# One splitter for each weight chunk, and small loads from another queue, in a three-layer mixture-of-experts program

## The chip, the cores and the metric

The kernel runs on one core of a Trainium2 chip. The metric is the device time of one execution in microseconds (us), the median of several runs.

## The reference

256 tokens of width 1024 in fp32 go through three layers. The first two form one block: a conditioning vector gives shift, scale and gate of each layer, a token mixer follows and then a mixture of experts. The third is a second block with another mixer.

```python
def first_block(x, c, ...):
    cond = jax.nn.silu(c)
    for layer in range(DEPTH):                        # 2
        mod = (cond @ ada_w[layer] + ada_b[layer])[:, None, :]
        shift1, scale1, gate1, shift2, scale2, gate2 = jnp.split(mod, 6, axis=-1)
        h = _rms(x, norm1_w[layer]) * (1 + scale1) + shift1
        ...
            y = _even_mixer(h, ...)                   # layer 0: window attention and gated linear attention
        ...
            y = _odd_mixer(h, ...)                    # layer 1: block attention
        x = x + gate1 * y
        h = _rms(x, norm2_w[layer]) * (1 + scale2) + shift2
        x = x + gate2 * _hier_moe(h, ...)             # 4 groups of 8 experts, hidden width 512
    return x

def second_block(x, attn_norm, w_in, ...):
    ...
        h = rmsnorm(x, attn_norm[layer])
        proj = h @ w_in[layer]
        ...
        o_nsa = nsa_mixer(...)                        # attention over compressed, selected, window keys
        o_hg = hgrn2_mixer(hg_q, hg_f, hg_i, lb)
        ...
        mixed = (gate_nsa * (o_nsa.astype(x.dtype) @ w_br_nsa[layer]) +
                 gate_hg * (o_hg @ w_br_hg[layer]))
        x = x + mixed @ w_out[layer]
        x = x + hier_moe(rmsnorm(x, ffn_norm[layer]), ...)
    return rmsnorm(x, final_norm)
```

## The kernel before, in words

One class, Net, writes the whole program. The stages follow each other: the even mixer (about 20 to 170 us of the trace), its experts, the odd mixer (about 684 to 835), its experts, the second block's mixer (about 1322 to 1545), its output projection and experts, and the last norm.

**Weights.** Almost all bytes are weights. They go into a ring of 19 slots of 1 MB (128 partitions x 2048 fp32). `plan` queues a load; `pump` (L182 to L194) issues queued loads on SP (SyncE) for as long as slots are free, with `dma_start` at L194. A slot is free when the last reader of the weights in it is done, and SP waits there.

**Splitting.** The mixers' matmuls run as three passes of a rounded format (fp32r), so each operand is a high part and a low part. For weights `prep` (L441) does this in chunks of two rows of blocks: ScalarE (ACT) casts 128x1024 to the high part `wh` at L461; VectorE (DVE) subtracts for the first half of the low part `wl` at L462, GpSimd (POOL) for the second half at L463, each 128x512. There are 120 such chunks, all in the mixers and the projections behind them; 112 are of this size, the others narrower. The high and low parts go to slots of the ring or to two buffers `wx`. `slab` (L468) takes one prepared chunk at a time and gives PE (TensorE) its matmuls (L258). The expert stages use their weights directly, without this split.

**Order.** Within a mixer `weave` (L213) interleaves generators: the projections (`stream`), the attention, the recurrent part. What a generator writes down lands on each engine's queue in that order, and each engine works through its queue in order. Copies out of PSUM go through `copy` (L249 on ACT, L251 on DVE), splits of activations through L254 (ACT) and L255 (DVE), transposes through `tr` (L268). In the attention of the second block L1284 to L1287 scale the exponentials of a row by the reciprocal of their sum, on DVE. In the odd mixer L1054 to L1063 are the softmax (L1058 the exponential on ACT, L1063 the scaling on DVE). L408 scales a selection matrix with the norm's coefficients at the start of a mixer, L631 applies a per-head norm, L798 gates the linear attention's output, L379 is a tiny power on POOL for the norms.

**Small loads.** 27 loads of constants and small weights stand on ACT's queue where a generator reaches them: `router` (L1619 to L1622, four loads, called in each of the three mixers' `stream`), `second_setup` (L1156, eleven loads, called in the odd mixer behind `router`), `nsa_prep` (L1165 and L1166, the two compression weights, into a slot of the ring), `hgrn` (L1335, the table `lvm`) and L1590 (the last norm's weight). A few loads of the first setup and of the biases stay on ACT in both kernels.

Of the kernel before, what the change touches and what calls it, by code (L numbers as in the profile page):

```python
# [9 lines left out]
FT = mybir.dt.float32  # L10
# [9 lines left out]
P = 128  # L20
D = 1024
KC = D // P
# [100 lines left out]
class Net:  # L123
# [322 lines left out]
    def prep(self, most=9):  # L446
        nc = self.nc
        while self.cq and len(self.ready) < min(most, len(self.wbufs) - 1):
            key, k, last = self.cq[0]
            if key not in self.live:  # L450
                self.pump()
                if key not in self.live:
                    return
            self.cq.pop(0)
            w = self.live[key]
            n = w.shape[2]
            src = w[:, k:k + 2]
            buf = self.wbufs[self.wi]
            self.wi = (self.wi + 1) % len(self.wbufs)
            wh, wl = (buf[:, 1024 * i:1024 * i + 2 * n].rearrange("p (k n) -> p k n", k=2) for i in range(2))  # L460
            nc.scalar.copy(wh, src)  # L461
            nc.vector.tensor_sub(wl[:, 0], src[:, 0], wh[:, 0].bitcast(FT))  # L462
            nc.gpsimd.tensor_sub(wl[:, 1], src[:, 1], wh[:, 1].bitcast(FT))  # L463
            self.ready.append((wh, wl))
            if last:
                self.done(key)
# [678 lines left out]
    def second_setup(self, g):  # L1145
        nc, A = self.nc, self.A
        self.S = {}
        for nm, src, shape in (
                ("k_rope", A["k_rope"], [P, 2 * T]), ("k_ropec", A["k_ropec"], [64, 60]), ("k_rot", A["k_rot"], [P, P]),
                ("k_csel", A["k_csel"], [30, P]), ("k_vmask", A["k_vmask"], [P, 512]),  # L1150
                ("pos", A["cmp_pos_2"][0].rearrange("(l q) d -> l (q d)", q=2), [16, P]),
                ("k_cmp", A["k_cmp"], [P, 64]), ("k_causal", A["k_causal"], [P, T]), ("k_scan", A["k_scan"], [P, T]),
                ("hn", A["hg_norm_2"].to_broadcast([P, P]), [P, P]),
                ("ll", A["hg_lb_logits_2"].rearrange("l (h p) -> (l h) p", p=P), [8, P])):
            self.S[nm] = g.tile(shape, FT, name=nm)
            nc.scalar.dma_start(self.S[nm], src)  # L1156

    def nsa_prep(self, g):
        nc, A = self.nc, self.A
# [2 lines left out]
        co, si = rp[:, :T], rp[:, T:]  # L1162
        vmk = vmk.rearrange("p (a b c) -> p a b c", a=4, b=2)
        wc = N["wc"]
        nc.scalar.dma_start(wc[:, 0], A["w_cmp_k_2"][0].rearrange("(l p) e -> p l e", p=P))  # L1165
        nc.scalar.dma_start(wc[:, 1], A["w_cmp_v_2"][0].rearrange("(l p) e -> p l e", p=P))  # L1166
        kr, vr = N["kr"], N["vr"]
        nc.gpsimd.memset(kr, 0.0)
        yield (0.0, 3.0)
        p = self.psum((P, 16))  # L1170
# [34 lines left out]
        p = self.psum((P, 64))  # L1205
# [10 lines left out]
        for b in range(2):  # L1216
            for gg in range(2):
                for par in range(2):
                    src = ks[64 * gg:64 * gg + 64, b]
# [98 lines left out]
    def hgrn(self, g, q8):  # L1318
        nc, A = self.nc, self.A
        q4 = lambda i: q8[i // 2][:, 1024 * (i % 2):1024 * (i % 2) + 1024]  # L1320
        h4 = lambda i: q4(i).rearrange("p (h t) -> p h t", h=4)
        k, b, q = (h4(i) for i in range(3))
# [9 lines left out]
        f = exs[0]  # L1332
        self.H = dict(k=k, b=b, q=q, v=v, gs=gs, f=f)
        lvm = g.tile([P, 7, 64], U32, name="lvm")
        nc.scalar.dma_start(lvm, A["k_levels"])  # L1335
        scan, ll = self.S["k_scan"], self.S["ll"]
        self.hn = self.S["hn"]
        nc.gpsimd.memset(att, 0.0)
# [1 line left out]
        p = self.psum((P, 8))  # L1340
# [72 lines left out]
        for t in range(NT):  # L1413
            p = self.psum()
# [6 lines left out]
        for c in range(3):  # L1421
            r0, t = 64 * (c % 2), c // 2
            p = self.psum()
# [9 lines left out]
        for t in range(NT):  # L1433
            po = self.psum()
            for h in range(4):
                o = po[:, P * h:P * h + P]
# [15 lines left out]
        for t in range(NT):  # L1452
            p = self.psum()
# [8 lines left out]
    def second(self, coeffs):  # L1462
        nc, tc = self.nc, self.tc
        with tc.tile_pool(name="sec", bufs=1, reuse_waits="tile") as g:
# [98 lines left out]
            def stream():  # L1563
# [23 lines left out]
                yield from branch(self.o[2:], 1)  # L1587
                self.release(3, reserve=3)
                coeffs()
                nc.scalar.dma_start(self.rows[1], self.A["final_norm_2"].rearrange("(o n) -> o n", o=1).to_broadcast([P, D]))  # L1590
                yield (5.0, 0.0)
                m = [(self.mx[0][:, k], self.mx[1][:, k]) for k in range(8)]
                yield from self.out_half(m[:4], False)
                yield from self.out_last(m[4:], False)

            self.weave(self.nsa_prep(g), self.nsa_attn(g, sc), self.hgrn(g, q8), stream())
        self.release(6)

# [15 lines left out]
    def router(self, l):  # L1614
        nc = self.nc
        wg, bg, we, be = self.moe_args(l)[0]
        wr = self.cp.tile([P, KC, 36], FT, name="wr", tag="wr")
        br = self.cp.tile([P, 36], FT, name="br", tag="br")
        nc.scalar.dma_start(wr[:, :, 0:4], wg.rearrange("(p k) n -> p k n", k=KC), allow_slow_non_contiguous=True)  # L1619
        nc.scalar.dma_start(wr[:, :, 4:36], we.rearrange("(p k) n -> p k n", k=KC), allow_slow_non_contiguous=True)  # L1620
        nc.scalar.dma_start(br[:, 0:4], bg.to_broadcast([P, 4]))
        nc.scalar.dma_start(br[:, 4:36], be.to_broadcast([P, 32]))  # L1622
        self.wr, self.br = wr, br

    def route_setup(self):
# [448 lines left out]
```

## Time and profile before

| | us |
|---|---|
| runs | 2068.37, 2071.49, 2070.86 (median 2070.86) |
| profiled execution, its own time | 2067.69 |
| its span in the trace | 2065.9 |
| PE busy | 1897.2 (92%) |
| DVE busy | 822.9 (40%) |
| ACT busy | 458.3 (22%) |
| POOL busy | 309.8 (15%) |
| read from memory | 722.48 MB, 350 GB/s over the span |

The shares are averages over stages that differ, so the profile is read by stretches of time. In a timeline row the first number is the start in us, the second the duration, "xN" a count of like instructions in a row, and the bracket the idle time of that engine just before and what ended it. "PE ps L258 <- DVE slot L462" reads: PE's instruction of L258 waited for DVE's of L462.

### The profile page before, as it was taken

The numbers are of one execution on the slowest core, as the hardware profiler recorded it, in microseconds if no ns is written. First come the engines' busy times: TensorE is split into PE (matmuls) and PEld (weight loads), VectorE is DVE, ScalarE is ACT, GpSimd is POOL, SyncE is SP. The second block draws the span as 40 slices with busy tenths as digits, with TensorE's granted clock in tenths as the row PEclk, the third lists the DMA queues.
The fourth block names the chain that finished last, engine by engine and source line by source line (L and its number), as shares of the span: only waits on it lengthen the run. The fifth ranks groups of instructions, "written<-read, shape, count | busy, mean of one in ns | idle before, by whom it ended". The sixth has DMA issues, their size and how long they took to land.

```text
span 2065.9 us, 25147 instructions
## 1 busy us (share of the span) xinstructions
PE 1897.2 (92%) x10032; PEld 1022.1 (49%) x10032; DVE 822.9 (40%) x1553; ACT 458.3 (22%) x838; POOL 309.8 (15%) x245
## 2 busy tenths in 40 slices
PE   6898999998989989999999889998899999999987
PEld 3655444343333657544433334586788443344333
DVE  3666433232322657623322222467666323222222
ACT  1424211111110443311111111254543111111111
POOL 1331000000000424000000000242443000000000
PEclk8998999999999999999999999999999999999999
DMA  8796999999999956799999999931357999999997
GB/s 314 274 312 251 375 422 421 420 421 422 421 420 405 367 211 242 303 401 421 421 421 421 421 421 421 342 106 42 131 191 268 379 421 421 420 421 421 421 421 287
DMA packets 157541, 725.29 MB, mean 351 GB/s; under 512 B 25305, under 2 KB 43087, under 8 KB 85225
## 3 DMA queue, kind: packets, MB, share of 16 engines
q1 hardware_dynamic: 139216, 716.84, 86.4%
q10 hardware_dynamic: 18201, 6.76, 1.3%
q8 instruction: 82, 1.34, 0.3%
q14 instruction: 42, 0.34, 0.0%
HBM read 722.48 MB, written 1.07 MB: 350 GB/s over the span
## 4 chain that ended last, share of the span: by engine, by line
DMA 23%; PE 19%; DVE 3%; issue 3%; ACT 2%; ACTq 0%; POOL 0%; POOLq 0%; SPq 0%; DVEq 0%
PE ps L258 18%; DMA slot<-moe_w 8%; DMA slot<-w_gate 5%; DMA slot<-w_up 4%; DMA slot<-w_down 2%; DMA more<-w_down 2%; DMA more<-w_up 2%; PE ps L268 1%; DVE slot L1287 1%; ACT slot L1275 1%; DMA slot<-w_in 0%; ACT slot L461 0%; DVE slot L462 0%; DVE hh L1861 0%; DVE wx L462 0%
## 5 line engine op out<-in xcount | busy, mean ns | idle before, releaser
L258 PE MATMUL ps<-slot,xg 128*64 128x512 f32 x2952 | 700.2, 599 | 47.5 <-DMA slot<-moe_w 34.3
L258 PEld LDWEIGHTS ps<-slot,xg 128*64 128x64 f32 x2952 | 225.0, 138 | 490.2 <-issue 381.2
L258 PE MATMUL ps<-slot 128*128 128x256 f32 (+8 forms) x2230 | 370.2, 327 | 11.5 <-DVE slot L462 9.0
L258 PE MATMUL ps<-slot,ht 128*64 128x512 f32 (+1 forms) x1592 | 341.7, 570 | 4.9 <-ACT ht L249 4.9
L258 PEld LDWEIGHTS ps<-slot 128*128 128x128 f32 (+3 forms) x2230 | 300.0, 186 | 72.2 <-issue 16.0
L1861 DVE SCALAR_TENSOR_TENSOR hh<-sg,ws,ps 128x512 f32<-128x512 f32 x48 | 54.3, 1130 | 603.6 <-PE ps L258 349.1
L258 PEld LDWEIGHTS ps<-slot,ht 128*64 128x64 f32 x1592 | 113.8, 137 | 198.1 <-issue 183.2
L1882 POOL TENSOR_TENSOR yl<-sg,yh 128x512 fp32r<-128x512 f32 (+1 forms) x68 | 82.4, 1211 | 862.5 <-ACT yh L1881 862.5
L463 POOL TENSOR_TENSOR slot<-slot 128x512 fp32r<-128x512 f32 (+2 forms) x108 | 163.5, 1531 | 279.5 <-ACT slot L461 247.3
L1908 DVE TENSOR_TENSOR x<-x,ps 128x512 f32<-128x512 f32 x180 | 113.6, 680 | 43.7 <-PE ps L258 41.5
L462 DVE TENSOR_TENSOR slot<-slot 128x512 fp32r<-128x512 f32 (+2 forms) x108 | 105.7, 992 | 57.3 <-ACT slot L461 54.6
L258 PEld LDWEIGHTS ps<-u,slot 128*128 128x128 f32 x864 | 105.6, 195 | 23.4 <-issue 17.0
L461 ACT CAST slot<-slot 128x1024 fp32r<-128x1024 f32 (+2 forms) x108 | 106.5, 1020 | 46.4 <-PE ps L258 24.8
L258 PE MATMUL ps<-u,slot 128*128 128x256 f32 (+1 forms) x864 | 111.0, 287 | 3.5 <-DVEq L1743 3.5
L1880 DVE TENSOR_TENSOR sg<-ps,ga 128x512 f32<-128x512 f32 (+1 forms) x68 | 44.9, 660 | 166.1 <-PE ps L258 155.8
L1857 ACT ACTIVATE sg<-ps 128x512 f32<-128x512 f32 x48 | 28.7, 597 | 325.7 <-PE ps L258 325.7
L1881 ACT CAST yh<-sg 128x512 fp32r<-128x512 f32 (+1 forms) x68 | 40.3, 593 | 251.7 <-DVE sg L1880 251.7
L258 PE MATMUL ps<-yh,pg 128*128 128x512 f32 (+1 forms) x204 | 85.5, 421 | 0.7 <-ACT yh L1881 0.7
L249 ACT COPY ht<-ps 128x512 f32<-128x512 f32 x48 | 28.1, 585 | 252.1 <-PE ps L268 251.9
L258 PE MATMUL ps<-yl,pg 128*128 128x512 f32 (+1 forms) x204 | 78.8, 389 | 4.3 <-POOL yl L1882 4.0
L399 ACT ACTIVATE xg<-ps,cf 128x256 f32<-128x256 f32 (+1 forms) x72 | 39.0, 542 | 172.6 <-PE ps L258 172.6
L1933 POOL TENSOR_TENSOR slot<-x,rows 128x512 f32<-128x512 f32 x2 | 2.6, 1276 | 460.2 <-DVE x L1929 460.2
(333 smaller groups left out, 1555.0 us busy)
## 6 DMA issues: line engine op xcount, KB each, us to landing
slot<-moe_w SPq DMA_DIRECT2D x376, 1024.0 KB, 19.8
slot<-w_gate SPq DMA_DIRECT2D x59, 1024.0 KB, 19.8
slot<-w_down SPq DMA_DIRECT2D x55, 1024.0 KB, 19.8
slot<-w_up SPq DMA_DIRECT2D x54, 1024.0 KB, 19.8
slot<-ada_w SPq DMA_DIRECT2D x48, 1024.0 KB, 9.0
slot<-w_in SPq DMA_DIRECT2D x20, 1024.0 KB, 7.4
slot<-odd_w_in SPq DMA_DIRECT2D x12, 1024.0 KB, 17.0
more<-w_up SPq DMA_DIRECT2D x10, 1024.0 KB, 16.1
```

The costliest lines, as they stand in the source:

```text
L249: self.nc.scalar.copy(out, in_)
L258: self.nc.tensor.matmul(out, lhsT=lhsT, rhs=rhs, start=start, stop=stop)
L399: self.nc.scalar.activation(out, p, AF.Identity, scale=a, bias=nb[:, k:k + 1])
L461: nc.scalar.copy(wh, src)
L462: nc.vector.tensor_sub(wl[:, 0], src[:, 0], wh[:, 0].bitcast(FT))
L463: nc.gpsimd.tensor_sub(wl[:, 1], src[:, 1], wh[:, 1].bitcast(FT))
L1857: nc.scalar.activation(sg, ps, AF.Silu)
L1861: nc.vector.scalar_tensor_tensor(ha.rearrange("s k p -> s p k"), st["sg", p].rearrange("s (p k) -> s p k", k=4), st["ws", p], ps.rearrange ...
L1880: nc.vector.tensor_mul(y, ps, self.ga[:, sl])
L1881: nc.scalar.copy(yh, y)
L1882: nc.gpsimd.tensor_sub(yl, y, yh.bitcast(FT))
L1908: nc.vector.tensor_add(self.x[:, t, sl], self.x[:, t, sl], ps)
```

## The change

The split of a chunk's low part becomes one DVE subtraction over the whole chunk (128x1024) in place of one half on DVE and one on POOL. The 27 small loads named above are issued by SP in place of ACT. Nothing else differs; lines behind L463 have numbers lower by one in the changed kernel.

```diff
--- before.py
+++ after.py
@@ -459,8 +459,7 @@
             self.wi = (self.wi + 1) % len(self.wbufs)
             wh, wl = (buf[:, 1024 * i:1024 * i + 2 * n].rearrange("p (k n) -> p k n", k=2) for i in range(2))
             nc.scalar.copy(wh, src)
-            nc.vector.tensor_sub(wl[:, 0], src[:, 0], wh[:, 0].bitcast(FT))
-            nc.gpsimd.tensor_sub(wl[:, 1], src[:, 1], wh[:, 1].bitcast(FT))
+            nc.vector.tensor_sub(wl, src, wh.bitcast(FT))
             self.ready.append((wh, wl))
             if last:
                 self.done(key)
@@ -1153,7 +1152,7 @@
                 ("hn", A["hg_norm_2"].to_broadcast([P, P]), [P, P]),
                 ("ll", A["hg_lb_logits_2"].rearrange("l (h p) -> (l h) p", p=P), [8, P])):
             self.S[nm] = g.tile(shape, FT, name=nm)
-            nc.scalar.dma_start(self.S[nm], src)
+            nc.sync.dma_start(self.S[nm], src)
 
     def nsa_prep(self, g):
         nc, A = self.nc, self.A
@@ -1162,8 +1161,8 @@
         co, si = rp[:, :T], rp[:, T:]
         vmk = vmk.rearrange("p (a b c) -> p a b c", a=4, b=2)
         wc = N["wc"]
-        nc.scalar.dma_start(wc[:, 0], A["w_cmp_k_2"][0].rearrange("(l p) e -> p l e", p=P))
-        nc.scalar.dma_start(wc[:, 1], A["w_cmp_v_2"][0].rearrange("(l p) e -> p l e", p=P))
+        nc.sync.dma_start(wc[:, 0], A["w_cmp_k_2"][0].rearrange("(l p) e -> p l e", p=P))
+        nc.sync.dma_start(wc[:, 1], A["w_cmp_v_2"][0].rearrange("(l p) e -> p l e", p=P))
         kr, vr = N["kr"], N["vr"]
         nc.gpsimd.memset(kr, 0.0)
         yield (0.0, 3.0)
@@ -1332,7 +1331,7 @@
         f = exs[0]
         self.H = dict(k=k, b=b, q=q, v=v, gs=gs, f=f)
         lvm = g.tile([P, 7, 64], U32, name="lvm")
-        nc.scalar.dma_start(lvm, A["k_levels"])
+        nc.sync.dma_start(lvm, A["k_levels"])
         scan, ll = self.S["k_scan"], self.S["ll"]
         self.hn = self.S["hn"]
         nc.gpsimd.memset(att, 0.0)
@@ -1587,7 +1586,7 @@
                 yield from branch(self.o[2:], 1)
                 self.release(3, reserve=3)
                 coeffs()
-                nc.scalar.dma_start(self.rows[1], self.A["final_norm_2"].rearrange("(o n) -> o n", o=1).to_broadcast([P, D]))
+                nc.sync.dma_start(self.rows[1], self.A["final_norm_2"].rearrange("(o n) -> o n", o=1).to_broadcast([P, D]))
                 yield (5.0, 0.0)
                 m = [(self.mx[0][:, k], self.mx[1][:, k]) for k in range(8)]
                 yield from self.out_half(m[:4], False)
@@ -1616,10 +1615,10 @@
         wg, bg, we, be = self.moe_args(l)[0]
         wr = self.cp.tile([P, KC, 36], FT, name="wr", tag="wr")
         br = self.cp.tile([P, 36], FT, name="br", tag="br")
-        nc.scalar.dma_start(wr[:, :, 0:4], wg.rearrange("(p k) n -> p k n", k=KC), allow_slow_non_contiguous=True)
-        nc.scalar.dma_start(wr[:, :, 4:36], we.rearrange("(p k) n -> p k n", k=KC), allow_slow_non_contiguous=True)
-        nc.scalar.dma_start(br[:, 0:4], bg.to_broadcast([P, 4]))
-        nc.scalar.dma_start(br[:, 4:36], be.to_broadcast([P, 32]))
+        nc.sync.dma_start(wr[:, :, 0:4], wg.rearrange("(p k) n -> p k n", k=KC), allow_slow_non_contiguous=True)
+        nc.sync.dma_start(wr[:, :, 4:36], we.rearrange("(p k) n -> p k n", k=KC), allow_slow_non_contiguous=True)
+        nc.sync.dma_start(br[:, 0:4], bg.to_broadcast([P, 4]))
+        nc.sync.dma_start(br[:, 4:36], be.to_broadcast([P, 32]))
         self.wr, self.br = wr, br
 
     def route_setup(self):
```

How it moves the instructions, at three places.

POOL in the second block's mixer (`slot` and `wx` are the buffers of the split chunks; L1383 and L1540 belong to the recurrent part). Before:

```order
L463 TENSOR_TENSOR wx<-slot,wx 128x512
L463 TENSOR_TENSOR slot<-slot 128x512 x4
L1383 TENSOR_TENSOR slot<-slot 128x16x32
L1383 TENSOR_TENSOR slot<-slot 128x32x16
L463 TENSOR_TENSOR wx<-slot,wx 128x512
L463 TENSOR_TENSOR slot<-slot 128x512 x2
L1383 TENSOR_TENSOR slot<-slot 128x64x8
L463 TENSOR_TENSOR slot<-slot 128x512
L1383 TENSOR_TENSOR slot<-slot 128x128x4
L463 TENSOR_TENSOR slot<-slot 128x512
L463 TENSOR_TENSOR wx<-slot,wx 128x512
L463 TENSOR_TENSOR slot<-slot 128x512
```

Now:

```order
L1223 COPY kd<-slot 64x256 x4
L1382 TENSOR_TENSOR slot<-slot 128x16x32
L1382 TENSOR_TENSOR slot<-slot 128x32x16
L1382 TENSOR_TENSOR slot<-slot 128x64x8
L1382 TENSOR_TENSOR slot<-slot 128x128x4
L1539 TENSOR_TENSOR slot<-slot,hn 128x512 x2
L1382 TENSOR_TENSOR slot<-slot 128x256x2
```

The subtractions are gone from POOL's queue, and what is left there, L1383 (now L1382) and L1540 (now L1539), follows directly. On DVE each L462 stands at its old place with 128x1024 in place of 128x512.

ACT in the odd mixer, behind the copies of `ga` and the four router loads (k_rope to ll are the constants of `second_setup`). Before:

```order
L1156 DMA k_rope<-k_rope 128x512
L1156 DMA k_ropec<-k_ropec 64x60
L1156 DMA k_rot<-k_rot 128x128
L1156 DMA k_csel<-k_csel 30x128
L1156 DMA k_vmask<-k_vmask 128x512
L1156 DMA pos<-cmp_pos 16x128
L1156 DMA k_cmp<-k_cmp 128x64
L1156 DMA k_causal<-k_causal 128x256
L1156 DMA k_scan<-k_scan 128x256
L1156 DMA hn<-hg_norm 128x128
L1156 DMA ll<-hg_lb_logits 8x128
L254 CAST slot<-ps 128x256 x3
```

Now, from the copies on:

```order
L249 COPY slot<-ps 128x512
L249 COPY ga<-ps 128x512 x2
L254 CAST slot<-ps 128x256 x3
L1057 ACTIVATE sc,den<-sc,mx 128x128
L1057 ACTIVATE sc,den<-sc,mx 128x256
L461 CAST slot<-slot 128x1024 x2
L249 COPY pT<-ps 128x384
```

The 15 loads stood between the copies and the casts L254; now the casts follow the copies. On SP these 15 stand behind the first of four loads of ada_w.

SP at the start of the second block's mixer (w_in, w_br_nsa and w_br_hg are the mixer's weights, lvm the table of levels). Before:

```order
L194 DMA slot<-w_in 128x4x512 x2
L194 DMA slot<-w_in 128x4x280 x2
L194 DMA slot<-w_in 128x4x512 x18
L194 DMA slot<-w_br_nsa 128x4x512 x2
L194 DMA slot<-w_br_hg 128x4x512 x2
```

Now:

```order
L194 DMA slot<-w_in 128x4x512 x2
L194 DMA slot<-w_in 128x4x280 x2
L194 DMA slot<-w_in 128x4x512 x2
L1164 DMA slot<-w_cmp_k 128x16x64
L1165 DMA slot<-w_cmp_v 128x16x64
L1334 DMA lvm<-k_levels 128x448
L194 DMA slot<-w_in 128x4x512 x4
L1618 DMA wr<-w_grp 128x8x4
L1619 DMA wr<-w_rtr 128x8x32
```

The two compression weights and the table stand behind the sixth load of w_in and ahead of the seventh; the router's loads stand behind the tenth, with two more for the biases, and then come the other twelve of w_in.

## Rows read from the trace of the kernel before

**Rows 1.** Stretches: us, then PE, PEld, DVE, ACT, POOL busy (instructions), clock, DMA share, GB/s.
```profile
100.00:150.00 50.00, 49.21 (x291) 28.75 (x289) 31.09 (x68) 13.22 (x16) 17.52 (x13) 1.00 0.98 314
300.00:600.00 300.00, 280.41 (x1336) 116.43 (x1332) 84.91 (x130) 36.89 (x63) 28.05 (x22) 0.99 1.01 421
700.00:750.00 50.00, 47.62 (x235) 34.16 (x234) 31.17 (x62) 19.47 (x34) 19.91 (x15) 1.00 0.56 204
1322.00:1545.00 223.00, 202.11 (x1610) 176.93 (x1609) 149.23 (x301) 108.46 (x198) 90.25 (x70) 0.95 0.38 128
```

**Rows 2.** What SP waited for in the whole span: us in total, times, longest.
```profile
SPq L194 <- DVE slot L462: 251.1, 34, 29.3
```

**Rows 3.** What PE waited for from 1322 to 1545 us, the second block's mixer.
```profile
PE ps L268 <- DVE slot L1287: 13.3, 9, 2.5
PE ps L258 <- DVE slot L251: 2.6, 1, 2.6
PE ps L258 <- DVE sel L408: 2.4, 2, 2.0
```

**Rows 4.** What PE waited for from 684 to 835 us, the odd mixer.
```profile
PE ps L268 <- DVE sc L1063: 7.6, 2, 6.3
PE ps L258 <- DVE slot L462: 3.4, 3, 2.9
```

**Rows 5.** What PE waited for from 40 to 170 us, the even mixer.
```profile
PE ps L258 <- DVE slot L462: 5.5, 4, 3.6
PE ps L268 <- DVE slot L798: 3.9, 1, 3.9
```

**Rows 6.** Single lines, duration of one in ns, min/median/max, first and last start, forms.
```profile
L462 DVE TENSOR_TENSOR slot<-slot x108: 426/693/1779, 43.1 to 1579.2; 128x512 fp32r<-128x512 f32 x101, 128x256 fp32r<-128x256 f32 x4, 128x280 fp32r<-128x280 f32 x3
...
L463 POOL TENSOR_TENSOR slot<-slot x108: 796/1718/1828, 43.0 to 1580.4; 128x512 fp32r<-128x512 f32 x101, 128x256 fp32r<-128x256 f32 x4, 128x280 fp32r<-128x280 f32 x3
...
L1287 DVE TENSOR_SCALAR slot<-slot,den x32: 273/341/1349, 1393.8 to 1468.2; 128x128 f32<-128x128 f32 x16, 128x256 f32<-128x256 f32 x16
...
L408 DVE TENSOR_SCALAR sel<-km,xr x6: 280/1284/1308, 17.7 to 1324.3; 128x128 f32<-128x128 f32 x6
...
L1407 DVE TENSOR_TENSOR slot<-slot x1: 1226/1226/1226, 1509.0 to 1509.0; 128x1024 f32<-128x1024 f32 x1
```

**Rows 7.** Timeline of DVE, POOL and PE around 1409 to 1421 us (start, duration, instruction).
```profile
1410.57 0.69 DVE L462 TENSOR_TENSOR slot<-slot 128x512 fp32r<-128x512 f32 x1 [1.86 <-ACT slot L461]
1411.52 1.46 DVE L462 TENSOR_TENSOR slot<-slot 128x512 fp32r<-128x512 f32 x1 [0.26 <-ACT slot L461]
...
1414.18 4.22 DVE L1287 TENSOR_SCALAR slot<-slot,den 128x128 f32<-128x128 f32 x8
...
1410.62 4.72 POOL L463 TENSOR_TENSOR slot<-slot 128x512 fp32r<-128x512 f32 x3 [4.28 <-ACT slot L461]
...
1415.47 0.33 PE L268 MATMUL ps<-km,slot 128*128 128x128 f32 x1 [1.87 <-DVE slot L1287]
1417.47 2.12 PE L268 MATMUL ps<-km,slot 128*128 128x128 f32 x7 [1.67 <-DVE slot L1287]
```

**Rows 8.** Timeline of ACT, DVE and PE around 743 to 764 us.
```profile
753.66 0.92 ACT L254 CAST slot<-ps 128x256 fp32r<-128x256 f32 x3 [7.53 <-DMA k_cmp<-k_cmp]
...
754.06 1.09 DVE L255 TENSOR_TENSOR slot<-ps,slot 128x256 fp32r<-128x256 f32 x3 [10.60 <-ACT slot L254]
...
762.08 0.87 PE L268 MATMUL ps<-km,sc 128*128 128x128 f32 x3 [6.31 <-DVE sc L1063]
```

**Rows 9.** Timeline of ACT at 1358 to 1364 us.
```profile
1361.83 2.00 ACT L461 CAST slot<-slot 128x1024 fp32r<-128x1024 f32 x2 [3.39 <-DMA wr<-w_rtr]
```

**Rows 10.** Timeline of SP at 1300 to 1345 us.
```profile
1304.73 37.58 SPq L194 DMA_DIRECT2D slot<-w_in  x11
```

**Rows 11.** Page, section 6: KB and us from issue to landing.
```profile
slot<-w_in SPq DMA_DIRECT2D x20, 1024.0 KB, 7.4
```

## The prediction

> **What bounds the kernel now.** I read the stretches first [rows 1]. From 300 to 600 us, inside a mixture-of-experts stage, the DMA engines are busy 1.01 of the time at 421 GB/s: there the loading of weights sets the pace, and nothing that DVE, ACT or POOL does matters. From 700 to 750 us, in the odd mixer, DMA is at 0.56, and from 1322 to 1545 us, in the second block's mixer, at 0.38, while PE is busy 202.11 of 223 us. In the mixers, then, PE and what PE waits for set the pace. Loads can't run ahead there, because they wait for ring slots: SP stood 251.1 us behind L462, the VectorE subtraction that reads a chunk of raw weights last but for POOL's [rows 2]. So a microsecond that PE gains in a mixer starts the next load-bound stage a microsecond earlier; the bytes behind it are the same, and I count it one for one to the end. From 100 to 150 us, in the even mixer, DMA is at 0.98 [rows 1], so there I count half.
>
> Next I read what PE waits for in each mixer [rows 3 to 5]. In the second block it is mostly L1287, the scaling of the attention rows (13.3 us in nine waits), then the copy L251 (2.6) and L408 (2.4). In the odd mixer it is L1063 (7.6, of which one wait is 6.3), L462 (3.4) and again L408 (its row reads as in the second block: 2.4 in two waits); in the even one L462 (5.5) and L798 (3.9).
>
> Then I asked why those DVE lines are late. Their durations are bimodal [rows 6]: L462 takes 693 ns in the median and up to 1779, L1287 from 273 to 1349, L408 from 280 to 1308, and POOL's half, L463, from 796 to 1828. The timeline at 1410 us shows why [rows 7]. DVE's first L462 starts at 1410.57 just before POOL's L463 and takes 0.69 us. The second starts while POOL is running and takes 1.46. POOL works through three L463 in 4.72 us, to 1415.34, and for that long DVE's small L1287 crawl, so that PE waits 1.87 and then 1.67 us. So in this trace DVE and POOL do not run side by side on these operands: whichever comes second waits for the other to end. POOL's half of each chunk is not free work; it is put in front of DVE's.
>
> **The change part by part.**
>
> *The subtraction.* It removes 120 L462 and 120 L463 (108 of each into ring slots [rows 6], 12 into the buffer wx) and adds 120 DVE subtractions of a whole chunk. The price of one: L1407 is a DVE tensor-tensor of 128x1024 f32 and takes 1.226 us [rows 6]. Per chunk that compares with 0.69 on DVE, and 1.7 us (L463's median 1718) in which the pair is occupied.
>
> Gain at the place of rows 7: the first new subtraction ends at 1410.57 + 1.23 = 1411.80, the second at 1413.03. Two small operations follow, for which I allow 0.55 us (an estimate: twice the shortest L1287), then L1287 at 0.27 each: the first is done about 1413.85. PE is free at 1415.47 - 1.87 = 1413.60, and then takes 0.33 for a transpose, more than an L1287 takes, so it isn't stopped again. Of the two waits, 3.5 us, 3.2 go. Elsewhere I cannot do it wait by wait, since behind a wait that goes stands the next dependency. L1383 and others stay on POOL and still collide, and the exps on ACT set when L1287 may start. I take two thirds of the waits that end in a DVE line that POOL lengthens; the ends are one third and all.
> Second mixer: L1287 and L408, 13.3 + 2.4 = 15.7, two thirds 10.5.
> Odd mixer: L1063, L462 and L408, 7.6 + 3.4 + 2.4 = 13.4, two thirds 8.9. In this the 6.31 us gap at 762.08 has a second cause, told below, and 4.2 of the 8.9 come from it.
> Even mixer: L462 and L798, 9.4, two thirds 6.3, and half of that 3.1 because of the DMA share.
>
> Cost: where L462 had run alone (0.69), the new subtraction takes 1.23, so +0.53, wherever somebody waits for DVE right then. I take nine places: seven waits on L462 [rows 4, 5] and two more in front of L1287 and L251. 9 x 0.53 = 4.8. Ends: none, and twice that.
>
> *The small loads.* 27 of them leave ACT's queue for SP's. The one that counts is a row of 15 in the odd mixer. Behind it ACT's L254 starts at 753.66 after 7.53 us in which ACT only issued, DVE's L255 had been idle 10.60, and PE's transpose at 762.08 stood 6.31 us [rows 8]. Of these 6.31 I count the two thirds above; the rest PE would wait for the scores. In the second mixer four router loads hold ACT for 3.39 us ahead of its casts [rows 9], and PE later stands 2.6 us for L251 [rows 3]. I take all of it, as the casts move by more than the gap. The other eight have no PE wait near them: nothing.
>
> Against that the Trainium skill, DMA: Bandwidth & Descriptors, section Issuing engines are not separate DMA queues, says that issuing from several engines saves only the time of initiating, usually small beside the DMA itself. By that the loads are worth nothing and the sum below is less by 4.2 + 2.6. The trace has 7.53 us of initiating in front of one waited-for instruction, so here I go by the row.
>
> On SP the loads are now in front of weight loads. In the odd mixer 15 issues (some 7.5 us, as on ACT) delay three ada_w loads; no row of PE waits there names a DMA [rows 4], DMA is at 0.56, so nothing. In the second mixer the loads of w_cmp_k, w_cmp_v and lvm sit behind the sixth w_in, and wait for their buffers. On ACT they were issued between 1334 and 1339; SP had issued eleven w_in from 1304.73 within 37.58 us [rows 10]. So the seventh w_in now goes out about 1339 and lands 7.4 us later [rows 11], near 1347. Its first cast is the second one of the group at 1361.83 [rows 9], about 1359.5 once ACT is early. Slack 12 us: nothing, and that slack is the cover.
>
> *Sum.* 10.5 + 2.6 + 8.9 + 3.1 - 4.8 = 20.3 us. The profiled run took 2067.69, so 2047.4. The median of the three runs, 2070.86, stands 3.2 above that run, and the forecast for a median is 2047.4 + 3.2, about 2050.5. Ends: all waits and no cost gives 15.7 + 2.6 + 13.4 + 4.7 = 36.4, or 2034.5; one third (5.2 + 4.5 + 1.6 = 11.3, nothing from L251) and a cost of 9.6 gives 1.7, or 2069.
>
> **The rivals.**
> *The next dependency takes over.* PE's waits on L1287 turn into waits on the exps or on its own order, and the recovered time is a third or less with the full cost: a gain of 2 to 7 us, 2064 to 2069. For it: DVE is busy 149.23 of 223 us in the second mixer and ACT only 108.46 [rows 1], so DVE is the chain already. Against it: nearly all of the two waits at 1413 to 1417 goes in the working above [rows 7].
> *The loads are worth nothing*, as in the rule named above: PE stands at 762 and at L251 for other reasons. Then 6.8 less: about 2057.
> *DVE becomes the bound: slower.* If the long L1287, L408 and L798 are long for another reason than L463 (POOL's remaining work, or the waiting for a semaphore), they stay long, and the new subtraction is only more DVE work. More than half of the 108 L462 of rows 6 ran at the median, so 54 x 0.53 = 28.6 us more; half of it on the path is 14.3, less 6.8 for the loads: +7.5, about 2078. It decides from 13 such halves on the path with nothing given back. Against it: the timeline has the long ones only beside L463.
> *SP is held*: w_cmp_k's buffer comes free 12 us later than I think and PE stands for a w_in. Each microsecond past the slack costs one; with 10 lost, 2060.
> That the change doesn't do what it says is ruled out by the order of the instructions.
>
> **How the numbers follow.** Forecast (2040 to 2062) 0.57, loads worth nothing 0.14, next dependency 0.14, DVE the bound 0.10, SP held 0.05. About 0.2% (4.1 us) is what a measurement here can tell from no change. Faster by more: the forecast, the loads case and SP held, and a third of the next-dependency case: 0.80. Within it: the rest of that case, 0.10. Slower: 0.10. The range leaves out the slower case and the far end of the gain: 2038 to 2067.
>
> **What would show it.** In the profile after: no L463; the new line at 1.2 us each and not 1.75, about 145 us in all; L1286 (the former L1287) with a median near 0.3 and none above 1 us except beside L1382; PE's waits on it under 5 us; ACT's L254 with no idle time behind DMA issues, and PE's stand before the transpose near 2 us; SP's wait behind L462 moved but not gone; the load-bound stretches still at 421 GB/s. It is wrong if L1286 stays long, if PE shows a new wait on ACT casts or on w_in, or if PE's waits vanish and the stage after does not start earlier.

## The result, and the profile after

The changed kernel takes 2037.18 us, the median of six runs (2033.84 to 2041.80), beside 2070.69 for the kernel before (six runs, 2067.48 to 2071.49). The ratio is 0.9843, with a 95% interval of 0.983 to 0.9857: about 33 us less, 29.6 to 35.2. The direction and the mechanism were forecast; the size was not: some 20 us were forecast, and the measured median lies 0.8 us below the low end of the stated range.

The page of the changed kernel:

```profile
span 2031.7 us, 24889 instructions
...
PE 1886.5 (93%) x10032; PEld 1013.7 (50%) x10032; DVE 811.5 (40%) x1553; ACT 458.4 (23%) x838; POOL 129.2 (6%) x125
...
POOL 0010011011101100011110011000000000000000
...
L462 DVE TENSOR_TENSOR slot<-slot 128x1024 fp32r<-128x1024 f32 (+2 forms) x108 | 128.5, 1210 | 43.9 <-ACT slot L461 43.6
...
PE 23%; DMA 21%; issue 2%; DVE 2%; ACT 1%; POOL 0%; POOLq 0%; ACTq 0%; SPq 0%; DVEq 0%
```

POOL's busy time falls from 309.8 to 129.2 us; DVE's does not rise, it falls from 822.9 to 811.5, though DVE now does the whole of 120 chunks. L462 takes 1.21 us on average, as the row of L1407 said [rows 6]. The line of slices is POOL's: in the three mixers almost nothing is left. The last row is the chain that ended last: DMA was in front with 23% before and is at 21% now, behind PE.

Stretches (us, then busy time of PE, PEld, DVE, ACT and POOL with the number of instructions, clock, DMA share, GB/s), for the expert stage, a part of the odd mixer and the second block's mixer, which starts 22 us earlier now:

```profile
250.00:550.00 300.00, 285.07 (x1380) 122.10 (x1378) 90.11 (x139) 39.02 (x67) 27.36 (x22) 0.99 1.01 421
684.00:734.00 50.00, 48.63 (x230) 36.58 (x231) 37.12 (x71) 21.15 (x37) 4.04 (x4) 1.00 0.84 307
1300.00:1523.00 223.00, 213.77 (x1730) 188.78 (x1729) 150.56 (x318) 114.11 (x206) 17.11 (x21) 0.98 0.46 154
```

The expert stage is as before, 1.01 and 421 GB/s [rows 1]. In the second mixer's 223 us PE is busy 213.77 where it was 202.11, at a clock of 0.98 where it was 0.95, and DVE 150.56 where it was 149.23.

What PE waits for in the odd mixer (680 to 835 us), and in the second block's (1290 to 1545); total, times, longest:

```profile
PE ps L268 <- DVE sc L1062: 1.3, 3, 0.8
PE ps L258 <- DVE slot L462: 1.3, 1, 1.3
PE ps L258 <- DVE slot L1036: 1.2, 2, 1.0
PE ps L258 <- DVE sel L408: 1.0, 1, 1.0
...
PE ps L268 <- DVE slot L1286: 4.8, 8, 2.2
PE ps L258 <- DVE sel L408: 1.3, 1, 1.3
PE ps L258 <- DVE qT L1142: 1.3, 1, 1.3
```

These answer to [rows 3] and [rows 4]: L1286 (the former L1287) 4.8 for 13.3 us, L1062 1.3 for 7.6, L462 1.3 for 3.4, L408 1.0 and 1.3 for 2.4 each; L251's 2.6 is 0.3. Two waits of more than 1 us are new or longer, L1142 with 1.3 and L1036 with 1.2 for 0.7 (L1037 before).

In the even mixer (40 to 170 us) less changes. L871 of the kernel before, which [rows 5] leaves out, then the same line (L870) and its neighbours now:

```profile
PE ps L268 <- DVE slot L871: 6.6, 1, 6.6
...
PE ps L268 <- DVE slot L870: 6.6, 1, 6.6
PE ps L258 <- DVE slot L462: 4.0, 4, 1.8
PE ps L268 <- DVE slot L797: 3.6, 1, 3.6
```

The place of [rows 7] now, DVE and then PE:

```profile
1383.40 2.62 DVE L462 TENSOR_TENSOR slot<-slot 128x1024 fp32r<-128x1024 f32 x2 [1.86 <-ACT slot L461]
1385.94 0.19 DVE L1283 RECIPROCAL den<-den 128x8 f32<-128x8 f32 x1
1386.17 0.17 DVE L1284 TENSOR_TENSOR den<-den,gt 128x8 f32<-128x8 f32 x1
1386.37 1.66 DVE L1286 TENSOR_SCALAR slot<-slot,den 128x128 f32<-128x128 f32 x8
...
1386.84 1.82 PE L268 MATMUL ps<-km,slot 128*128 128x128 f32 x8
```

Two subtractions take 2.62 us, the two small operations 0.4, and eight L1286 take 1.66 where they took 4.22. PE's eight transposes run in one piece without a wait.

The place of [rows 8] now, ACT, DVE and PE:

```profile
739.68 0.37 ACT L254 CAST slot<-ps 128x256 fp32r<-128x256 f32 x1
740.35 0.37 ACT L254 CAST slot<-ps 128x256 fp32r<-128x256 f32 x1 [0.30 <-PE ps L258]
...
740.08 0.42 DVE L255 TENSOR_TENSOR slot<-ps,slot 128x256 fp32r<-128x256 f32 x1 [3.15 <-ACT slot L254]
...
749.49 0.61 PE L268 MATMUL ps<-km,sc 128*128 128x128 f32 x3 [0.27 <-DVE sc L1062]
```

ACT's casts start right behind the copies, and PE's stand is 0.27 us for 6.31.

PE runs the same 10032 matmuls in the same order in both kernels, so the nth can be set beside the nth, and the difference split into PE's idle time ahead of matmuls and the time that they take. Worked out so from the two traces, from the first matmul on:

| matmuls | stage | idle, us | busy, us |
|---|---|---|---|
| 0 to 1100 | even mixer | +0.8 | -5.5 |
| 1100 to 3050 | its experts | -0.8 | +2.3 |
| 3050 to 3800 | odd mixer | -11.1 | -3.7 |
| 3800 to 5900 | its experts | -0.1 | -2.7 |
| 5900 to 7600 | second block's mixer | -11.7 | -3.0 |
| 7600 to 10031 | the rest | +0.1 | +1.9 |
| sum | | -22.8 | -10.7 |

So in these two profiles two thirds of the gain are waits of PE, and one third is PE itself being faster: its busy time on the page falls from 1897.2 to 1886.5 us. A second profile of the changed kernel, taken later, gives -21.7 and -6.4. The second number thus moves by several us from one execution to another.

### The profile page after: what moved, and what is told of

Its sections match the earlier page's. It is cut to its first block, busy times and chain, and to the rows that moved or that the text cites. A ratio compares the mean times of both kernels' runs of the same rounds, so it can differ in the third digit from the quotient of the medians.

```text
span 2031.7 us, 24889 instructions
## 1 busy us (share of the span) xinstructions
PE 1886.5 (93%) x10032; PEld 1013.7 (50%) x10032; DVE 811.5 (40%) x1553; ACT 458.4 (23%) x838; POOL 129.2 (6%) x125
## 5 line engine op out<-in xcount | busy, mean ns | idle before, releaser
L258 PE MATMUL ps<-slot,xg 128*64 128x512 f32 x2952 | 698.3, 598 | 46.6 <-DMA slot<-moe_w 33.4
L258 PE MATMUL ps<-slot 128*128 128x256 f32 (+8 forms) x2230 | 360.1, 320 | 9.8 <-DVE slot L462 5.3
L258 PEld LDWEIGHTS ps<-slot 128*128 128x128 f32 (+3 forms) x2230 | 292.8, 181 | 67.6 <-issue 15.6
L462 DVE TENSOR_TENSOR slot<-slot 128x1024 fp32r<-128x1024 f32 (+2 forms) x108 | 128.5, 1210 | 43.9 <-ACT slot L461 43.6
L249 ACT COPY ht<-ps 128x512 f32<-128x512 f32 x48 | 28.1, 585 | 251.7 <-PE ps L268 251.2
L1884 DVE TENSOR_TENSOR yl<-ps,yh 128x512 fp32r<-128x512 f32 (+1 forms) x34 | 22.5, 660 | 93.5 <-ACT yh L1883 92.5
L258 PEld LDWEIGHTS ps<-yh,pg 128*128 128x128 f32 x204 | 38.5, 189 | 34.3 <-issue 23.9
```

Of the source, the lines that this page charges most:

```text
L249: self.nc.scalar.copy(out, in_)
L258: self.nc.tensor.matmul(out, lhsT=lhsT, rhs=rhs, start=start, stop=stop)
L462: nc.vector.tensor_sub(wl, src, wh.bitcast(FT))
L1884: nc.vector.tensor_sub(yl, ps, yh.bitcast(FT))
```

## The experiments

Each run is compared with runs of the kernel before on the same chip: 2071.19 us for the first four below, 2070.47 for more work on DVE, 2069.86 for the three with the even mixer's stands, and 2071.78 for the other four.

**The subtraction alone.** The loads stay on ACT; only the split is changed:

```diff
-            nc.vector.tensor_sub(wl[:, 0], src[:, 0], wh[:, 0].bitcast(FT))
-            nc.gpsimd.tensor_sub(wl[:, 1], src[:, 1], wh[:, 1].bitcast(FT))
+            nc.vector.tensor_sub(wl, src, wh.bitcast(FT))
```

> Theory (the loads' issue time on ACT and POOL's half are two separate causes): the one-piece subtraction alone takes most of the 33.5 us; PE's waits on L1287 and L408 go as in the changed kernel, but PE's stand before the transposes in the odd mixer (6.3 us before, 0.27 after) and the one before L251 (2.6) stay at least half: 2043 to 2046 us. Rival 1 (issuing queue is worth nothing): 2037, no difference from the changed kernel. Rival 2 (the two parts only work together, since ACT's casts feed the subtraction): over 2055.

Measured 2049.72 us, ratio 0.99 (0.9882 to 0.9917): 21.5 us less. PE's waits in the odd mixer:

```profile
PE ps L268 <- DVE sc L1062: 7.6, 3, 6.5
PE ps L258 <- DVE slot L462: 1.3, 1, 1.3
```

The 6.5 us stand is still there, and the waits on L462 are gone as far as in the changed kernel. Both rivals fall: the loads are worth something, and the parts do not need each other. The time is 4 us above the expected band, so the loads are worth more than thought.

**The loads alone.** The split stays as before, all 27 loads go to SP:

```diff
-            nc.scalar.dma_start(self.S[nm], src)
+            nc.sync.dma_start(self.S[nm], src)
...
-        nc.scalar.dma_start(wr[:, :, 0:4], wg.rearrange("(p k) n -> p k n", k=KC), allow_slow_non_contiguous=True)
+        nc.sync.dma_start(wr[:, :, 0:4], wg.rearrange("(p k) n -> p k n", k=KC), allow_slow_non_contiguous=True)
```

> Theory: PE's stand before the transposes in the odd mixer falls to about 2 us and the one before L251 goes, all waits on L1287 and L408 stay: a gain of 7 to 9 us, 2062 to 2064. Rival 1 (issuing queue is worth nothing): 2070. Rival 2 (the loads carry the surplus over the 20 us that were forecast): a gain of 15 or more, 2055.

Measured 2059.85 us, ratio 0.9948 (0.9934 to 0.9963): 11.3 us less, 2 us beyond the expected band. With the 21.5 of the other part this makes 32.8, against 33.5 for both together: they add. The odd mixer's and the second mixer's waits:

```profile
PE ps L258 <- DVE slot L462: 3.4, 3, 2.9
...
PE ps L268 <- DVE sc L1063: 1.2, 1, 1.2
...
PE ps L268 <- DVE slot L1287: 13.2, 9, 2.4
```

The wait on L1063 is down from 7.6 to 1.2 (the 6.31 us stand is wholly gone), while L462's 3.4 and L1287's 13.2 stand where they were. So each part removes its own waits.

**Only the 15 loads of the odd mixer.**

```diff
-            nc.scalar.dma_start(self.S[nm], src)
+            nc.sync.dma_start(self.S[nm], src)
...
+        eng = self.nc.sync if l == 1 else self.nc.scalar
...
-        nc.scalar.dma_start(wr[:, :, 0:4], wg.rearrange("(p k) n -> p k n", k=KC), allow_slow_non_contiguous=True)
+        eng.dma_start(wr[:, :, 0:4], wg.rearrange("(p k) n -> p k n", k=KC), allow_slow_non_contiguous=True)
...
```

> Only the 15 loads of the odd mixer go to SP. Theory: the gain of the loads in the odd mixer alone, 5 to 6 us, 2065; the second mixer's stand before L251 stays at 2.6. Rival (all 27 loads matter through the shared DMA bookkeeping on SP): much less than the run with all 27, 2069.

Measured 2063.00 us, ratio 0.9962 (0.995 to 0.9975): 8.2 us less, where 5 to 6 were expected. That leaves some 3 us for the other twelve, which agrees with the 2.6 us before L251.

**POOL reads again.** The changed kernel, with POOL's half back, into a scratch tile:

```diff
             nc.vector.tensor_sub(wl, src, wh.bitcast(FT))
+            nc.gpsimd.tensor_sub(self.decoy[:, :n], src[:, 1], wh[:, 1].bitcast(FT))
...
```

> The changed kernel, and POOL again subtracts the second half of each chunk as before, into a scratch tile that nobody reads. Theory (POOL's reading excludes DVE): L1286 and L408 are again over 1 us beside it, PE's waits on them return, and since DVE now does the whole chunk as well the time goes past the kernel before less its load gain: 2060 to 2080. Rival (before, consumers waited for POOL's result or DVE was slow for another reason; nobody reads the scratch tile): 2037 to 2041.

Measured 2098.31 us, ratio 1.0137 (1.0115 to 1.0158): 61 us more than the changed kernel, 27 more than the kernel before, and 18 above the expected band. No result is waited for here, and yet the pattern of [rows 7] is back (DVE, POOL, PE; L1289 is the old L1287):

```profile
1422.82 3.46 DVE L462 TENSOR_TENSOR slot<-slot 128x1024 fp32r<-128x1024 f32 x2 [1.85 <-ACT slot L461]
...
1426.43 1.00 DVE L1287 TENSOR_TENSOR den<-den,gt 128x8 f32<-128x8 f32 x1
1427.46 4.34 DVE L1289 TENSOR_SCALAR slot<-slot,den 128x128 f32<-128x128 f32 x8
...
1422.93 5.82 POOL L463 TENSOR_TENSOR decoy<-slot 128x512 f32<-128x512 f32 x3 [4.33 <-ACT slot L461]
...
1428.88 0.33 PE L268 MATMUL ps<-km,slot 128*128 128x128 f32 x1 [3.55 <-DVE slot L1289]
1430.88 2.12 PE L268 MATMUL ps<-km,slot 128*128 128x128 f32 x7 [1.67 <-DVE slot L1289]
```

While POOL is in its three subtractions, the small operation ahead of the scalings (here L1287, in the changed kernel L1284) takes 1.00 us for 0.17, the eight scalings take 4.34 for 1.66, and PE waits 3.55 and 1.67. The rival falls. POOL's reading also keeps ring slots from SP (22.0 us of SP's waits end in it), but PE waits for loads as little as in the changed kernel (33.7 us on moe_w for 33.4, 4.7 on ada_w for 4.6), so late loads are not the cause.

Which operations of DVE are held up can be worked out from the trace of the kernel before, by setting those that overlap an L463 beside those that overlap no work of POOL. L631, with both operands in SBUF (the on-chip memory in which the tiles lie), takes 1.77 us for 0.69 in the median. L251 and L330, with an operand in PSUM, take 0.68 for 0.69: they are not held up.

**POOL only writes.** Nearly as busy as before the change (255.3 us for 309.8), but with two memsets in place of the subtraction:

```diff
             nc.vector.tensor_sub(wl, src, wh.bitcast(FT))
+            nc.gpsimd.memset(self.decoy, 0.0)
+            nc.gpsimd.memset(self.decoy, 0.0)
...
```

> The changed kernel, with two memsets of a 128x512 scratch tile on POOL at each chunk: POOL is as busy as before the change in the mixers, but reads nothing. Theory (it is POOL's reading that shuts DVE out): L462 and L1286 keep their lengths, 2036 to 2041 us. Rival (any work of POOL on SBUF shuts DVE out, or a busy POOL queue delays L379 and L1382 and so PE): 2050 and more.

Measured 2039.51 us, ratio 0.984 (0.982 to 0.9861): no difference from the changed kernel that can be told.

```profile
L464 POOL MEMSET decoy<- 128x512 f32 x120 | 63.7, 531 | 6.9
...
1361.52 1.22 DVE L462 TENSOR_TENSOR slot<-slot 128x1024 fp32r<-128x1024 f32 x1
...
1361.42 0.53 POOL L464 MEMSET decoy<- 128x512 f32 x1
1362.00 0.52 POOL L463 MEMSET decoy<- 128x512 f32 x1
...
L1290 DVE TENSOR_SCALAR slot<-slot,den x32: 269/347/1356, 1375.6 to 1441.6; 128x128 f32<-128x128 f32 x16, 128x256 f32<-128x256 f32 x16
```

The first row is one of two such lines of the kernel: 240 memsets, 127 us of POOL. They wait for no data, so POOL runs them in rows behind its own work and not always beside the chunk they were written for. Still 45 of the 112 whole-chunk L462 overlap a memset, as in the rows from 1361 us, and their median is 1.22 us, that of the others 1.22; in the run before, 78 of 112 overlap POOL's subtraction, with a median of 2.25 us for 1.22 (worked out from the two traces). Of the 32 scalings the memsets met only three, so on those the run says little. For the subtractions, then, it is not a busy POOL that costs, but a POOL that reads; its subtraction reads two operands, and whether one would do it was not tried. The long L1290 (up to 1356 ns) stand beside L1544 and L1386, the gating and the exponent differences that POOL still does.

The Trainium skill, SBUF — State Buffer, section Who interferes with whom, says the same: a DVE instruction with two inputs in SBUF contends with a GpSimd instruction that reads SBUF, not with one that only writes it. By the same section of the Trainium skill a DVE instruction in a mode that uses two ports, which tensor_scalar (the scalings) can enter, contends with GpSimd too, and the one that issues first holds the shared ports for its whole length. The two runs agree with the first, with 61 us against 2; with the second agree the eight L1289 that take 4.34 us beside POOL's subtractions for 1.66.

**More work on DVE itself.** The same scratch subtraction as in the run where POOL reads again, but on DVE:

```diff
             nc.vector.tensor_sub(wl, src, wh.bitcast(FT))
+            nc.vector.tensor_sub(self.decoy[:, :n], src[:, 1], wh[:, 1].bitcast(FT))
...
```

> The changed kernel, and behind each subtraction DVE does another one of 128x512 into a scratch tile that nobody reads: 0.69 us more on DVE at each of 120 chunks, 83 us in all, with POOL out of the way. Theory (DVE time at a chunk seldom lies on the path; the forecast charged nine places of 72): about an eighth of it shows, 10 us, 2047 to 2051. Rival (the two-halves run, 18 us more of DVE for 5 to 7 us, is the true rate): 25 to 33 us, 2062 to 2072.

Measured 2075.22 us, ratio 1.0025 (1.0015 to 1.0034): 38 us more than the changed kernel, above both expected bands.

```profile
L463 DVE TENSOR_TENSOR decoy<-slot x108: 419/685/1785, 44.3 to 1588.7; 128x512 f32<-128x512 f32 x101, 128x256 f32<-128x256 f32 x4, 128x280 f32<-128x280 f32 x3
...
PE ps L268 <- DVE slot L1289: 10.0, 7, 3.0
```

120 instructions of 0.69 us (108 in the row, 12 more into wx) are 83 us, and 46% of them arrive at the end, far more than the nine places of 120 that the forecast charged (the 72 of the expectation has no source in the rows). Not all of it is DVE on the path: set beside the profile of the changed kernel, PE's idle time grew by 25.2 us (30% of the 83) and its busy time by 15.6. And the same work costs 38 us on DVE, but 61 us on POOL.

**Two halves on DVE.** Both halves as separate instructions of 128x512:

```diff
-            nc.vector.tensor_sub(wl, src, wh.bitcast(FT))
+            nc.vector.tensor_sub(wl[:, 0], src[:, 0], wh[:, 0].bitcast(FT))
+            nc.vector.tensor_sub(wl[:, 1], src[:, 1], wh[:, 1].bitcast(FT))
```

> The changed kernel, with the DVE subtraction written as two halves of 128x512, each 0.69 us by the row of L462 before, 1.38 together against 1.23. Theory (DVE's length is not on the path in most places; PE takes a chunk's halves one after the other): within 3 us of the changed kernel, 2036 to 2040. Rival (the added 0.53 us per chunk that the forecast charged at nine places is real, so 0.15 more at each of 120 chunks shows as well): 2040 to 2050.

Measured 2044.73 us (2037.43 to 2049.18), ratio 0.9863 (0.9836 to 0.989), 7.5 above the changed kernel by the medians, with intervals that overlap. The median lies in the rival's band, but the run is inconclusive by itself; at the 46% of the last run, 18 us more on DVE would be 8.

**PE kept busy in one stand.** The kernel before, with dummy matmuls ahead of the transposes of the fourth head in the odd mixer:

```diff
+                if h == 3:
+                    self.warm(6)
                 p = self.psum((P, w))
                 for b in range(3):
                     self.tr(p[:, P * b:P * b + P], sc[:, P * b:P * b + P])
```

> The kernel before, with six dummy matmuls of 476 columns (about 3.7 us) put into PE's 6.3 us stand ahead of the transposes in the odd mixer, so that PE is idle for less while everything else waits as before. Theory (the granted clock falls because PE stood, and part of the gain of the change is PE running faster behind the stands that went): the granted clock of the 20 us behind stays at 1.00 (0.91 and 0.83 in stretches of the kernel before) and the time falls by 1 to 2 us, 2069. Rival (the clock falls at its own times): the clock rows as before and the time the same or 0 to 1 us longer, 2071 to 2072.

Measured 2068.35 us, ratio 0.9983 (0.9971 to 0.9996): 3.4 us less, with more work, and more than the 1 to 2 us expected. The stretches from 754 and 764 us, first the kernel before, then this one:

```profile
754.00:764.00 10.00, 3.69 (x14) 2.80 (x13) 5.98 (x15) 4.40 (x11) 2.94 (x2) 0.75 0.89 339
764.00:774.00 10.00, 10.00 (x52) 6.63 (x51) 4.73 (x8) 3.82 (x7) 4.05 (x3) 0.91 1.05 389
```

```profile
754.00:764.00 10.00, 8.51 (x33) 4.78 (x35) 5.88 (x15) 4.66 (x10) 2.95 (x2) 1.00 0.93 343
764.00:774.00 10.00, 10.00 (x60) 6.78 (x58) 5.93 (x10) 4.88 (x8) 4.58 (x3) 1.00 1.05 388
```

In the 20 us that hold the 6.3 us stand and what follows it the granted clock was 0.75 and 0.91; with 1.49 us of the stand left it stays at 1.00. The six matmuls behind the transposes, before and in this run:

```profile
762.60 2.91 PE L258 MATMUL ps<-slot 128*128 128x512 f32 x6
...
762.29 1.63 PE L258 MATMUL ps<-slot 128*128 128x512 f32 x6
```

In the changed kernel the stretch behind its place, 754 to 774 us, is at 1.00 as well. So here part of PE's own time is bought back by its not standing, which is the rival refuted and the theory shown for one place.

**Less on POOL.** The changed kernel, with ten more two-input operations moved from POOL to DVE, among them L1539:

```diff
-            nc.gpsimd.tensor_sub(ev[:, :, :h], ref, bv[:, :, :h])
+            nc.vector.tensor_sub(ev[:, :, :h], ref, bv[:, :, :h])
...
-                nc.gpsimd.tensor_mul(gv, gv, self.hn[:, None, :].to_broadcast([P, 4, P]))
+                nc.vector.tensor_mul(gv, gv, self.hn[:, None, :].to_broadcast([P, 4, P]))
```

> The changed kernel, with the remaining two-input tensor operations that POOL still does in the even and in the second block's mixer (the gating by the norm weights and the first half of the exponent differences, ten instructions) moved to DVE. Theory (what is left of the shutting out, 1.35 us L1286 beside L1539 and PE's 2.2 us wait on it, goes): 2 to 4 us below the changed kernel, 2033 to 2035. Rival (DVE is now the bound, and ten more instructions of 0.7 us cost what they free): 2037 to 2042.

The longest wait on L1286 that is left stands beside L1539 in the changed kernel (POOL, then PE):

```profile
1430.83 2.66 POOL L1539 TENSOR_TENSOR slot<-slot,hn 128x512 f32<-128x512 f32 x2 [16.11 <-ACT slot L1537]
...
1433.69 2.59 PE L268 MATMUL ps<-km,slot 128*128 128x128 f32 x10 [2.21 <-DVE slot L1286]
```

Measured 2034.97 us, ratio 0.9819 (0.9795 to 0.9844). The longest L1286 goes from 1356 to 354 ns:

```profile
L1286 DVE TENSOR_SCALAR slot<-slot,den x32: 280/314/354, 1368.1 to 1432.9; 128x128 f32<-128x128 f32 x16, 128x256 f32<-128x256 f32 x16
```

The mechanism is as expected; the 2.2 us of gain lie within the spread of the runs.

**The even mixer's stands filled**, alone and together with the last edit, and the changed kernel once more beside them:

```diff
+        self.warm(4)
         for t in range(NT):
             p = self.psum()
             for h in range(4):
                 self.tr(p[:, P * h:P * h + P], ob[:, t, h])
...
+            if n:
+                self.warm(7)
             po = self.psum()
```

> The changed kernel, with dummy matmuls in PE's two longest stands that are left, in the even mixer: four ahead of the transposes that wait for L797 (3.6 us), seven ahead of those that wait for L870 (6.6 us). Theory (PE's clock falls because it stands): the granted clock of 150 to 170 us, 0.51 and 0.63 in the changed kernel, stays near 1.00, the matmuls there run at full speed, and the time falls by 2 to 5 us against the changed kernel. Rival (the even mixer's end is set by the loads, DMA share near 1, or the clock falls anyway): no difference beyond 1 us.

> The two edits together, fewer two-input operations on POOL and the dummy matmuls in the even mixer. Theory (separate places, so they add): 4 to 7 us below the changed kernel, 2030 to 2033, the fastest of all. Rival (one of them is nothing): 2034 to 2036.

> The changed kernel beside the two others on the same chip: 2037, as measured before; a value over 2 us away would mean that chips differ by more than the edits do.

Measured 2037.33 (ratio 0.9841, 0.9822 to 0.9861), 2036.49 (0.9842, 0.9824 to 0.986) and 2039.47 (0.9845, 0.9827 to 0.9862). The clock in the even mixer's end, the changed kernel and then the one with the stands filled:

```profile
150.00:160.00 10.00, 3.44 (x17) 2.34 (x17) 5.03 (x22) 8.77 (x32) 0.00 (x0) 0.51 1.03 411
160.00:170.00 10.00, 8.83 (x33) 5.04 (x32) 4.99 (x17) 3.23 (x10) 0.00 (x0) 0.63 0.45 162
```

```profile
150.00:160.00 10.00, 9.00 (x33) 4.51 (x32) 5.40 (x23) 9.28 (x34) 0.00 (x0) 1.00 1.03 408
160.00:170.00 10.00, 8.68 (x36) 4.88 (x37) 5.38 (x16) 3.94 (x10) 0.00 (x0) 0.83 0.61 223
```

The clock rises from 0.51 and 0.63 to 1.00 and 0.83, as the theory has it, but the time does not follow: 2.1 us below the changed kernel, not to be told from nothing. The two edits together miss their band of 2030 to 2033 us, and the repeat of the changed kernel stands 2.3 us above its first measurement, which its expectation took as the sign that chips differ by more than these edits do. So a higher clock in one place need not arrive at the end. By the method of the table, with the 22 dummy matmuls counted to the even mixer, this run's trace gains 6.3 us in that mixer, where the two profiles of the changed kernel gain 4.7 and 0.9, and 11.9 in the second block's mixer, where they gain 14.7 and 13.3; where the expected gain went is open. No version was shown to beat the changed kernel.

## Why the prediction was right, and where it was short

**Right.** The diagnosis held step by step. DVE and POOL shut each other out on these reads (the runs in which POOL reads and in which it only writes), so giving all to DVE does not make DVE busier. L462 is at 1.21 us for the 1.23 taken from L1407. The two waits of [rows 7] went entirely, 3.2 of 3.5 us forecast. The waits on L1287 fell by 8.5 us, 8.9 forecast (two thirds of 13.3); those that stay above 1 us stand beside L1539 as well as beside L1382, which the prediction named alone. The three loads in front of the seventh w_in cost nothing: from 1290 to 1545 us no row of PE's waits names w_in. The expert stages stayed at 421 GB/s, and the gain of each mixer was carried to the end.

The rivals fell: the loads alone gave 11.3 us and not nothing, so the rule of the Trainium skill (DMA: Bandwidth & Descriptors, Issuing engines are not separate DMA queues) that the prediction weighed, by which issuing elsewhere saves little, does not decide a case in which 15 issues stand ahead of one cast; DVE did not become the bound; SP was held longer at its three loads than thought (13 us, from 1294 to 1307.7, for 5), but the seventh w_in still went out early enough, at 1307.7 us where the forecast's 1339 less the 22 us of the earlier start is 1317.

**Short, by 13 us.** The separate runs give the terms of the sum:

| term | forecast, us | measured alone, us |
|---|---|---|
| 27 loads | 4.2 + 2.6 = 6.8 | 11.3 |
| of these the odd mixer's 15 | 4.2 | 8.2 |
| subtraction, after its cost of 4.8 | 10.5 + 4.7 + 3.1 - 4.8 = 13.5 | 21.5 |

Three steps failed. The first is the loads' term, "the rest PE would wait for the scores": two thirds of the 6.31 us stand were counted, and all of it went (0.27 left, and 0.00 with the loads alone). Without the issues ACT's first cast follows the copies at once; I had no row that showed the scores to be late and should have taken the whole. In the trace of the 15 loads alone PE's idle time in the odd mixer fell by 6.6 us; the rest of the 8.2 is not idle time of that mixer.

The second is a term that the sum does not have. It adds only PE's idle time, and that was nearly right: 20.3 us against 22.8 and 21.7 in the two profiles, in part by luck, as the odd mixer gave more than forecast (11.1 us for 8.9 before any cost) and the even mixer less (nothing for 3.1). But PE's matmuls themselves took 10.7 us less (6.4 in the second profile), at a mean granted clock of 0.982 (0.979) where it was 0.974. The kernel before showed it: 0.95 over its last mixer [rows 1] while the expert stage had 0.99. That the clock rose with the change is no accident of one execution: its mean was 0.968 to 0.976 in the 50 executions of the kernel before on record, and 0.978 to 0.984 in the 11 of the changed kernel. And the two runs that make PE stand more go the other way: against the changed kernel's first profile idle and busy time grew by 46.7 and 14.0 us where POOL reads again, by 25.2 and 15.6 where DVE does more. That standing causes part of it is shown by experiment at one place, the stand filled with dummy matmuls. For the rest it is argued only; the run with the even mixer's stands filled speaks for caution, and the size of the term stays open: the same split gives +0.1 us of busy time for the subtraction alone and -3.5 for the loads alone, in one profile each.

The third is the subtraction's net term, 13.5 us for 21.5. In the trace of the subtraction alone PE's idle time fell by 18.1 us, so the term was too small as idle time already. Its two parts cannot be told apart by the runs made. The cost's "nine places" are not borne out by the run with more work on DVE, in which 46% of added DVE time shows at the end; but that work stood behind the subtraction, so it does not measure the cost. If the cost was above 4.8 us, the relief was larger than two thirds of the waits by as much again; and the forecast's relief without any cost, 18.3 us, would fit the 18.1 as well. As I read it, both sizes suffer from one mistake: I set the relief (a part of PE's waits) against the cost (0.53 us where L462 had run alone) as two lists, where DVE's total time was nearly the same before and after (822.9 and 811.5 us). What changed was where DVE's time stands: before, behind POOL's row of subtractions (three at the place of [rows 7]) and so in front of exactly those small operations that PE waits for; now, within the chunk's own subtraction.

The even mixer gave no idle time at all (+0.8 for -3.1 forecast less cost): its long stands on L871 and L798, 6.6 and 3.9 us, are the same in the changed kernel but for 0.3 (6.6 and 3.6), and the second had been counted as if POOL lengthened it. The wait on L462 fell from 5.5 to 4.0 us only, and waits on L350 and on ACT's L249 grew by 2.4.

## What to carry to other kernels

When two engines that shut each other out split one job, look at what else the second engine's instructions delay: here POOL's half of a chunk, done "beside" DVE, cost more (61 us for a result that nobody read) than the same half added to DVE (38 us). A short operation with a bimodal duration, five times its minimum beside one line of another engine, is the sign in the profile. And a row of DMA issues on a compute engine's queue is a delay like any other: read what stands behind it, and move it to a queue on which nobody waits.

## What was not expected of the hardware

POOL's writing is not quite free for DVE either: the three scalings of 128x128 that stood beside memsets took 322, 704 and 575 ns, where the other 13 took 269 to 286, and all six L408 took 382 ns or more, where the shortest of the changed kernel took 279, though the time did not show it. And filling PE's stands with dummy matmuls kept its granted clock higher in both places tried (1.00 for 0.75 and 0.91, and 1.00 and 0.83 for 0.51 and 0.63), yet paid 3.4 us in the one (0.9971 to 0.9996 of the time before) and nothing that could be told in the other.
